# Up-projection of a ConvFFN in seven block products, with weight sums made by accumulating transfers

## The chip, the core and the metric

One core of a Trainium2 chip. The metric is the device time in microseconds of one execution. TensorE (PE) multiplies, VectorE (DVE), ScalarE (ACT) and GpSimd (POOL) work on tiles of 128 partitions, and SyncE (SP) issues most transfers. Each engine works through its own list of instructions in order; semaphores tie the lists together. A transfer that POOL issues goes through POOL's queue of descriptors, one that SP issues through SP's.

## What is computed

One layer of a hybrid decoder, for 512 prompt tokens and 8 single-token samples, 520 columns in all; the model width is 2048, the feed-forward width 5632. Cut to what matters here:

```python
h = rmsnorm(x, ln_mix_pre)
proj = h @ w_in                          # 2048 x 6160
...                                      # windowed attention and gated delta rule
mix = concatenate([att, dn_out]) @ w_out # 2048 x 2048
x = x + rmsnorm(mix, ln_mix_post)
h = rmsnorm(x, ln_ffn_pre)
up, ffn_new = causal_dwconv(h @ w_ffn_in, ffn_buf, ffn_conv_w)   # 2048 x 11264, width 3
gate, val = split(up + ffn_conv_b, 2)
f = (gelu(gate) * val) @ w_ffn_out                               # 5632 x 2048
x = x + rmsnorm(f, ln_ffn_post)
```

The sample caches, shifted by one row, are outputs too (128 copies of up to 1 MB from HBM to HBM).

## The kernel before

Features lie on partitions and tokens on columns. Every product of float32 values is made of three matmuls on a rounded high part and a low part: high × high, high × low and low × high. A weight tile `raw` (128 x 1024, 512 KB) is loaded by SP (line 111) and split in two steps of 128 x 512: a cast on ScalarE (line 127, `hi`) and a subtraction on VectorE (line 128, `lo`). The operand tiles `xa` and `xb` hold the high and low parts for 256 and 264 of the 520 columns (halves A and B). `gemm` (lines 152 to 162) issues the matmuls (line 160): for a tile of 128 output features 16 k-blocks × 3 × 2 halves = 96.

Stage 3, the FFN, begins when the output projection's last matmuls end, near 978 us. The loop takes 11 parts of four pairs. Pair f is gate tile f and value tile 44 + f: two `u_tile` calls (192 matmuls), whose results are scaled by R2, the row of inverse norms (line 1114), into tiles U. Then the depthwise convolution (first tap on ScalarE, line 1122; two taps each on VectorE, line 1124), the gelu (line 1133), gate times value on VectorE (line 1134), and the split of the product into the down-projection's operand. After each part the down-projection of the part before it runs (`ffn_out`, 384 matmuls) and adds into `yacc` (line 1188). The last part's down-projection goes by halves of the tokens, with the output's norm behind it. In the first part half A of the tokens goes first, so that the norm of half B (`mid2`) is made meanwhile. `shift` issues the cache copies on SP, three per pair.

What sets the order: a scheduler lays out each engine's list at build time, `HI()` marks work that is to go early, and weight units are prefetched two ahead (`LOOK`), through 3 raw, 5 high and 5 low buffers. Within an engine nothing overtakes.

Of the kernel before, what the change touches and what calls it, by code (L numbers as in the profile page):

```python
# [18 lines left out]
T = 520  # L19
NB4 = 11  # L20
TAGS = ("bankS", "bankT", "bankP", "bankX")
NCV = 5
NA, NB = 256, 264
# [16 lines left out]
def trunk(ctx, tc, I, O):  # L40
# [13 lines left out]
    wraw = enter(pool("wraw", 3))  # L54
    whi = enter(pool("whi", 5))
    wlo = enter(pool("wlo", 5))
    xsA = enter(pool("xsA", 16))
    xsB = enter(pool("xsB", 16))
    rrow = enter(pool("rrow", 1))
    dram = enter(tc.tile_pool(name="dram", bufs=1, space=bass.MemoryType.DRAM))  # L60
    gps = enter(tc.tile_pool(name="gps", bufs=2, space=bass.MemoryType.PSUM))
    sps = enter(tc.tile_pool(name="sps", bufs=4, space=bass.MemoryType.PSUM))
    turn = [0]

    def bank(tag=None):
# [26 lines left out]
    def ffn_units(p):  # L92
        u = []
        for f in range(4 * p, 4 * p + 4):
            u += [I["w_ffn_in"][f], I["w_ffn_in"][44 + f]]
        return u
    units += ffn_units(0) + ffn_units(0)
    for p in range(1, NP):
        units += ffn_units(p)
        units += [I["w_ffn_out"][p - 1, g].rearrange("p a b c -> p (a b) c") for g in range(4)]  # L100
    for _ in range(1):
        units += [I["w_ffn_out"][NP - 1, g].rearrange("p a b c -> p (a b) c") for g in range(4)]
# [5 lines left out]
    def emit_half(u, hf):  # L108
        with HI():
            raw = wraw.tile([128, 8, 128], F32, name="raw")  # L110
            lastw[0] = Q.dma_start(raw, units[u][:, hf * 8:hf * 8 + 8, :])
            if u >= len(units) - 4:
                # the last part is used twice: kept whole where the FFN's operand lay
                for q in range(4):
                    b = hf * 8 + q * 2
                    t = xsA.tile([128, 2, NA], F32R, name="xa") if q % 2 else xsB.tile([128, 2, NB], F32R, name="xb")
                    r = raw[:, q * 2:q * 2 + 2, :].rearrange("p a b -> p (a b)")
                    S.copy(t[:, 0, 0:256], r)  # L118
# [27 lines left out]
    def wblk(u, b):  # L146
        if u >= len(units) - 4:
            return wt[u, "b", b]
        hi, lo = wt[u, b // 4]
        return hi[:, b % 4, :], lo[:, b % 4, :]  # L150

    def gemm(blks, X, ks, parts="AB"):
        ps = gps.tile([128, 1024], F32, name="ps")
        n = len(ks)
        for i, k in enumerate(ks):
            wh, wl = wblk(*blks[i])
            for j, (w, b) in enumerate(((wh, 0), (wh, 1), (wl, 0))):
                for part in parts:
                    o, w_ = SEG[part]
                    PE.matmul(ps[:, 256 + o:256 + o + w_], w, X[k][part][:, b, :],  # L160
                              start=(i == 0 and j == 0), stop=(i == n - 1 and j == 2))
# [12 lines left out]
    def norm_row(dst, acc, n, wp):  # L174
        """dst = (mean over features + eps)^-1/2 replicated on all partitions, from squares added over k-tiles."""
        cn, k = (128, 2) if n == 256 else (88, 3)
# [70 lines left out]
    def bias_tables():  # L247
        rb = Pd.tile([32, H], F32, name="rb")
        B.dma_start(rb, I["rel_bias"])
        for dst, o, n in ((FD, 0, 640), (FS, 640, 400)):  # L250
# [4 lines left out]
            for a in range(0, n, 512):  # L255
# [3 lines left out]
                if n == 640:  # L259
                    # the scores of the prompt are kept with the opposite sign  # L260
# [25 lines left out]
    def b_tile(ct, ps, early):  # L286
        U = Pd.tile([128, 3 + T], F32, name="cv", bufs=NCV)
        V.memset(U[:, 0:3], 0.0)
        with HI():
            if early:  # L290
                S.copy(U[:, 3:], ps[:, 256:776])
                V.tensor_mul(U[:, 3:], U[:, 3:], R1)
            else:
                V.tensor_mul(U[:, 3:], ps[:, 256:776], R1)
# [31 lines left out]
    # gates: rows 0..7 beta, rows 32..39 the decay  # L326
# [5 lines left out]
    def gates(ps):  # L332
# [5 lines left out]
        with HI():  # L338
            S.copy(ga, ps[0:40, 256:776])
# [22 lines left out]
    def gate_cols():  # L362
# [4 lines left out]
        # the samples' decay and beta on all partitions  # L367
# [30 lines left out]
    def col_sums(c, o, keep):  # L398
        """squared norms of q (o = 0) or k (o = 4), tokens of a chunk on partitions."""
# [147 lines left out]
    def scan(c):  # L547
# [48 lines left out]
        # state  # L596
# [12 lines left out]
        # outputs  # L609
# [32 lines left out]
    def over_partitions(rows):  # L642
        """sums over the partitions, on all of them."""
# [4 lines left out]
    def sample_dn():  # L648
# [16 lines left out]
        # partitions (sample, value head, half of dk)  # L665
# [80 lines left out]
    def rows_of(src, last):  # L746
        """[128 d, (h, b)] -> DRAM [b][h][d]: the queries, or the last row of a shifted cache."""
# [636 lines left out]
```

## Time and profile before

| | |
|---|---|
| median of three runs | 2528.92 us (2526.8 to 2529.82) |
| profiled execution, span | 2524.7 us |
| TensorE busy | 2445.2 us (97%), 20080 matmuls |
| VectorE, ScalarE, POOL busy | 1478.5 (59%), 983.2 (39%), 206.7 us (8%) |
| moved by transfers | 469.46 MB, mean 186 GB/s |

The page gives the span of one execution and no other time of it; the runs lie 2 to 5 us above. In a row of the groups, the first number after the bar is the busy time of all, the second the mean of one in ns, and behind the next bar stands the engine's idle time just before them with what ended it. In a row of transfers the last number is the median time from issue to landing.

### The profile page before, as it was taken

The numbers are of one execution on the slowest core, as the hardware profiler recorded it, in microseconds if no ns is written. First come the engines' busy times: TensorE is split into PE (matmuls) and PEld (weight loads), VectorE is DVE, ScalarE is ACT, GpSimd is POOL, SyncE is SP. The second block draws the span as 40 slices with busy tenths as digits, with TensorE's granted clock in tenths as the row PEclk, the third lists the DMA queues.
The fourth block names the chain that finished last, engine by engine and source line by source line (L and its number), as shares of the span: only waits on it lengthen the run. The fifth ranks groups of instructions, "written<-read, shape, count | busy, mean of one in ns | idle before, by whom it ended". The sixth has DMA issues, their size and how long they took to land.

```text
span 2524.7 us, 49670 instructions
## 1 busy us (share of the span) xinstructions
PE 2445.2 (97%) x20080; PEld 2424.1 (96%) x20080; DVE 1478.5 (59%) x3246; ACT 983.2 (39%) x2096; POOL 206.7 (8%) x470
## 2 busy tenths in 40 slices
PE   8499999998999999999999999999999999999996
PEld 7499999997999999999999999999999999999996
DVE  7379755676896567855454544445454545444467
ACT  6153244683335556632232323232323323232344
POOL 1120211212110000100000000000000000000000
PEclk9799999999999999999999999999999999999998
DMA  5663532559984567965564736364555546463753
GB/s 184 148 226 126 186 114 87 164 187 242 247 218 132 187 197 228 328 228 194 184 203 143 244 134 217 128 242 145 208 179 190 197 155 231 138 226 115 264 170 103
DMA packets 119061, 469.46 MB, mean 186 GB/s; under 512 B 20032, under 2 KB 39408, under 8 KB 116784
## 3 DMA queue, kind: packets, MB, share of 16 engines
q1 hardware_dynamic: 93648, 393.60, 46.1%
q0 software_dynamic: 25184, 72.69, 10.5%
q8 instruction: 158, 2.59, 0.4%
q14 instruction: 71, 0.58, 0.1%
HBM read 432.40 MB, written 167.97 MB: 238 GB/s over the span
## 4 chain that ended last, share of the span: by engine, by line
PE 85%; DMA 5%; DVE 4%; ACT 3%; issue 2%; another core or an unknown queue 2%; POOL 0%; SPq 0%; DVEq 0%; POOLq 0%; ACTq 0%
PE ps L160 80%; DMA pc<-in_cache_k_dram 2%; ACT prod L697 1%; DVE dtmp L706 1%; DMA raw<-in_w_out_dram 1%; DMA X1D<-x 1%; DMA raw<-in_w_ffn_out_dram 1%; PE bankX L513 1%; PE bankP L513 1%; DVE lo L128 0%; DVE sjk L783 0%; PE bankT L513 0%; PE bankS L513 0%; DMA out_s_rec_dram<-pc 0%
## 5 line engine op out<-in xcount | busy, mean ns | idle before, releaser
L160 PE MATMUL ps<-xb,hi 128*128 128x264 f32 x4640 | 1191.2, 287 | 0.0
L160 PE MATMUL ps<-xa,hi 128*128 128x256 f32 x4640 | 1181.2, 283 | 9.1 <-ACT xa L170 8.6
L127 ACT CAST hi<-raw 128x512 fp32r<-128x512 f32 x868 | 533.5, 619 | 1194.0 <-PE ps L160 1120.3
L160 PEld LDWEIGHTS ps<-xa,hi 128*128 128x128 f32 x4640 | 861.4, 190 | 14.3 <-ACT xa L170 8.6
L160 PEld LDWEIGHTS ps<-xb,hi 128*128 128x128 f32 x4640 | 861.4, 189 | 5.0 <-issue 2.7
L128 DVE TENSOR_TENSOR lo<-raw,hi 128x512 fp32r<-128x512 f32 x868 | 594.3, 689 | 462.5 <-ACT hi L127 460.7
L160 PE MATMUL ps<-xb,lo 128*128 128x264 f32 x2320 | 666.3, 287 | 3.1 <-DVE lo L128 1.5
L160 PE MATMUL ps<-xa,lo 128*128 128x256 f32 x2320 | 656.8, 283 | 0.0
L160 PEld LDWEIGHTS ps<-xb,lo 128*128 128x128 f32 x2320 | 438.2, 189 | 6.2 <-DVE lo L128 3.6
L160 PEld LDWEIGHTS ps<-xa,lo 128*128 128x128 f32 x2320 | 439.1, 189 | 0.8 <-issue 0.5
L160 PE MATMUL ps<-actB,hi 128*128 128x264 f32 x1280 | 337.1, 284 | 0.0
L160 PE MATMUL ps<-actA,hi 128*128 128x256 f32 x1280 | 333.3, 281 | 0.6 <-DVE yacc L1188 0.6
L160 PEld LDWEIGHTS ps<-actA,hi 128*128 128x128 f32 x1280 | 241.1, 188 | 0.8 <-ACT xb L118 0.8
L160 PEld LDWEIGHTS ps<-actB,hi 128*128 128x128 f32 x1280 | 240.5, 188 | 0.0
L1188 DVE TENSOR_TENSOR yacc<-yacc,ps 128x520 f32<-128x520 f32 (+2 forms) x176 | 113.8, 646 | 182.0 <-PE ps L160 180.5
L160 PE MATMUL ps<-actB,lo 128*128 128x264 f32 x640 | 181.7, 284 | 0.0
L160 PE MATMUL ps<-actA,lo 128*128 128x256 f32 x640 | 180.2, 282 | 0.0
L1124 DVE SCALAR_TENSOR_TENSOR gt<-U,cols,gt 128x512 f32<-128x512 f32 x176 | 131.9, 750 | 23.0 <-ACT gt L1122 20.9
L1140 POOL COPY pu<-U 128x2 f32<-128x2 f32 x88 | 49.7, 565 | 1136.6 <-DVE U L1114 1136.4
L1114 DVE TENSOR_TENSOR U<-ps,R 128x520 f32<-128x520 f32 (+2 forms) x92 | 61.1, 664 | 137.8 <-PE ps L160 137.7
L160 PEld LDWEIGHTS ps<-actA,lo 128*128 128x128 f32 x640 | 121.4, 190 | 0.0
L160 PEld LDWEIGHTS ps<-actB,lo 128*128 128x128 f32 x640 | 120.4, 188 | 0.0
(517 smaller groups left out, 2156.9 us busy)
## 6 DMA issues: line engine op xcount, KB each, us to landing
raw<-in_w_ffn_in_dram SPq DMA_DIRECT2D x192, 512.0 KB, 4.0
raw<-in_w_in_dram SPq DMA_DIRECT2D x98, 512.0 KB, 4.8
raw<-in_w_ffn_out_dram SPq DMA_DIRECT2D x88, 512.0 KB, 4.2
raw<-in_w_out_dram SPq DMA_DIRECT2D x64, 512.0 KB, 4.0
pc<-in_cache_k_dram POOLq DMA_DIRECT2D x24, 512.0 KB, 8.7
pc<-in_cache_v_dram POOLq DMA_DIRECT2D x24, 512.0 KB, 8.5
pc<-in_state_rec_dram POOLq DMA_DIRECT2D x16, 512.0 KB, 4.9
out_s_win_k_dram<-in_cache_k_dram SPq DMA_DIRECT2D x8, 1020.0 KB, 9.9
```

The source lines that it names most:

```text
L127: S.copy(hi, r)
L128: V.tensor_sub(lo, r, hi.bitcast(F32))
L160: PE.matmul(ps[:, 256 + o:256 + o + w_], w, X[k][part][:, b, :], start=(i == 0 and j == 0), stop=(i == n - 1 and j == 2))
L513: PE.matmul(p[:, j * 128:j * 128 + 128], lhs(4 * g + j), rhs(4 * g + j), start=True, stop=True)
L697: S.activation(dst[:, k], src(k), AF.Identity, scale=kqd[:, j, pc * 8 + k:pc * 8 + k + 1])
L706: V.tensor_reduce(dst, pr.rearrange("p k v -> p v k"), axis=AX.X, op=OP.add)
L1114: return V.tensor_mul(u, p, R2[:, o:o + w])
L1124: V.scalar_tensor_tensor(dst, U[:, j:j + 512], fwc(j, f), dst, op0=OP.mult, op1=OP.add)
L1140: G.tensor_copy(pu[:, s, i, :], U[:, 512:514])
L1188: ev = V.tensor_add(yacc[:, m, o:o + w], yacc[:, m, o:o + w], ps[:, 256 + o:256 + o + w])
```

## The change

The weights of pair f are seen as a 2 x 2 block matrix: rows are halves of the 2048 input features (8 k-blocks each), columns are gate and value: B11, B21 for the gate, B12, B22 for the value. The tokens' operand is a 2 x 2 block matrix too: rows are the halves of tokens (now 260 and 260), columns the feature halves. The four result blocks are made of seven products instead of eight. The operand sums A11, A12, A22, S1 to S4 are made once, in `mid2`, with R2 multiplied in; the weight sums are made for each pair. A product is 24 matmuls of 128 x 260 (line 1235).

The weight sums are transfers of POOL that add in flight (line 1153): the raw tile X holds a block, is cast and subtracted (`hl`, lines 1138 to 1142, now on 128 x 1024 at once), then the next block is added onto it from HBM, and so on: B11, + B12 (T1), + B22 (T2), + B21 (the last). Y holds B22, then B22 + B12. That is four adding transfers a pair.

Pairs below 16 have their two gate products (A11 with B11, A12 with B21) made ahead of the loop and kept in HBM (`PD`); they stand beside the making of half B's operands. Such a pair has five products in the loop, the others have seven.

The gated results go to HBM (`ACT`, line 1256) and the whole down-projection follows as sweeps of two parts, with PSUM adding over eight k-blocks (line 1413). The last part's weights are loaded twice. The gate times value multiply goes from VectorE to POOL (line 1255).

```diff
-NA, NB = 256, 264
+NA, NB = 260, 260
+EARLY = 16
...
-        norm_row(R2[:, o:o + w], acc3[:, :, :w], w, wk)
+        r2 = wk.tile([128, NB], F32, name="r2", bufs=1)
+        norm_row(r2, acc3, w, wk)
...
+        for i in range(4):
+            h1, h2 = scale(i), scale(4 + i)
+            put("A22", i, h2, xsB)
+            s = wk.tile([128, 2, w], F32, name="sd", bufs=2)
+            V.tensor_sub(s, h1, h2)
+            yield
+            a1, a2 = whole("A11", i), whole("A12", i)
+            V.tensor_sub(h1, a1, h1)
+            put("S3", i, h1, sxp)
+            put("S1", i, s, xsB)
...
+    wrx = enter(pool("wrx", 2))
+    whl = enter(pool("whl", 4))
...
+    def hl(raw):
+        t = whl.tile([128, 2, 8, 128], F32R, name="hl")
+        S.copy(t[:, 0], raw)
+        V.tensor_sub(t[:, 1], raw, t[:, 0].bitcast(F32))
+        return t
...
+    def wadd(t, src):
+        B.dma_start(t, src, accum_op=OP.add)
...
+    def pair_jobs(f):
+        def b11():
+            pre(f)
+            X = PRE[f][0]
+            t = hl(X)
+            wadd(X, wblock(f, 0, 1))
+            return t
...
+        def t1():
+            pre(f + 1)
+            X = PRE[f][0]
+            t = hl(X)
+            wadd(X, wblock(f, 1, 1))
+            return t
+
+        def t2():
+            X = PRE[f][0]
+            t = hl(X)
+            wadd(X, wblock(f, 1, 0))
+            return t
...
+        if f < EARLY:
+            jobs.extend([b22, t1, t2, last(1), last(0)])
+        else:
+            jobs.extend([b11, b22, t1, t2, last(1), last(2), last(0)])
...
+    JLOOK = 3
...
+    def product(p, X, first=True):
+        w = next_w()
+        n = 0
+        for a, b in ((0, (0, 1)), (1, (0,))):
+            for k in range(8):
+                for c in b:
+                    PE.matmul(p[:, 0:NA], w[:, a, k, :], X[k][:, c, :], start=first and n == 0, stop=n == 23,
...
-        V.tensor_mul(gt, gt, vt)
...
+        G.tensor_mul(gt, gt, vt)
+        Q.dma_start(ACT[f], gt)
...
+        pe = bank("bankX")
+        product(pe, XC["S4"])
+        v = small("v")
+        with HI():
+            S.copy(v, pe[:, :NA])
+        pd = fbank("bd")
+        product(pd, XC["S1"])
+        pb = fbank("bb")
+        product(pb, XC["S2"])
+        u2, u3 = small("u2", 1), small("u3", 1)
+        with HI():
+            V.tensor_add(u2, u, pb[:, :NA])
+            G.tensor_sub(v, v, u2)
+        pc = fbank("bc")
+        product(pc, XC["S3"])
...
+        product(pc, XC["A22"], first=False)
+        with HI():
+            V.tensor_add(gb_, u2, pc[:, :NA])
+        gated(f, Ug, Uv, pst)
+        shift(3)
...
+    sweeps = [(2 * i, 2 * i + 1) for i in range(5)] + [(10,)]
+    runs = [(s, "AB") for s in sweeps[:-1]] + [(sweeps[-1], "A"), (sweeps[-1], "B")]
```

How the instructions stand on the engines that the weights pass through. In the rows DMAHW is a wait for a transfer of SP, DMASW one for a transfer of POOL. First ScalarE's list in the middle of the FFN, before; `hi<-raw` is the weights' cast and `gt` the convolution and the gelu:

```order
L127 CAST hi<-raw 128x512 [waits DMAHW7_49,PE_49,Activation_49]
L127 CAST hi<-raw 128x512 [waits PE_49,Activation_49]
L127 CAST hi<-raw 128x512 [waits DMAHW3_49,PE_49,Activation_49]
L1122 ACTIVATE gt<-U,cols 128x512 [waits DVE_49,Pool_49]
L127 CAST hi<-raw 128x512 [waits PE_49,Activation_49]
L1133 ACTIVATE gt<-gt 128x512 [waits DVE_49]
L127 CAST hi<-raw 128x512 [waits DMAHW4_49,PE_49,Activation_49]
```

And the same list in the change, one of the pairs from 16 on; `rx` is X, `ry` is Y, `rz` is B21:

```order
L1341 COPY U<-ba 128x260 [waits PE_49]
L1243 ACTIVATE gt<-U,cols 128x512 [waits DMAHW3_49,DVE_49,Activation_49]
L1243 ACTIVATE gt<-U,cols 128x512 [waits Pool_49]
L1318 COPY u<-ba 128x260 [waits PE_49]
L1254 ACTIVATE gt<-gt 128x512 [waits DVE_49]
L1323 COPY v<-bankX 128x260 [waits PE_49]
L1140 CAST hl<-rx 128x1024 [waits DMASW3_49]
L1140 CAST hl<-rx 128x1024 [waits DMASW5_49]
L1140 CAST hl<-ry 128x1024 [waits DMASW4_49]
L1140 CAST hl<-rz 128x1024 [waits DMAHW5_49]
L1140 CAST hl<-rx 128x1024 [waits DMASW6_49,DVE_49,PE_49]
L1140 CAST hl<-rx 128x1024 [waits DMAHW3_49,DVE_49,PE_49]
```

Before, the casts wait for SP's loads and for free buffers and lie between the convolution's steps. Now the casts of T1 and T2 stand directly behind one another and behind the copy of S4's result, and three of the six wait for transfers of POOL.

ScalarE's list in the change for a pair below 16, from the gelu of the pair before it to the next pair's:

```order
L1254 ACTIVATE gt<-gt 128x512 [waits DVE_49]
L1140 CAST hl<-rx 128x1024 [waits DMASW1_49,Activation_49]
L1140 CAST hl<-ry 128x1024 [waits DMASW0_49,Activation_49]
L1140 CAST hl<-rx 128x1024 [waits DMASW3_49,PE_49]
L1140 CAST hl<-ry 128x1024 [waits DMAHW2_49,PE_49,Activation_49]
L1140 CAST hl<-rx 128x1024 [waits DMASW2_49,DVE_49,PE_49]
L1323 COPY v<-bankX 128x260 [waits PE_49,Pool_49]
L1243 ACTIVATE gt<-U,cols 128x512 [waits DMAHW1_49,DMAHW0_49,DVE_49]
```

Its casts are T2, Y's second, X's last, then B22 and T1 of the next pair; here T2 stands behind a gelu, and the next pair's B22, a plain load, behind X's last.

POOL's list before, from one pair to the next:

```order
L1118 MEMSET U 128x2 [waits DVE_49,Activation_49,Pool_49]
L1140 COPY pu<-U 128x2 [waits DVE_49]
L1141 COPY su<-U 128x8
```

And in the change, one of the pairs from 16 on:

```order
L1255 TENSOR_TENSOR gt<-gt 128x512 [waits DMAHW6_49,Activation_49]
L1153 DMA rx<-in_w_ffn_in_dram 128x1024 [waits DMASW7_49,DVE_49]
L1153 DMA rx<-in_w_ffn_in_dram 128x1024 [waits DMASW1_49,DVE_49]
L1331 TENSOR_TENSOR v<-v,u_19039 128x260 [waits DVE_49]
L1258 COPY pu<-U 128x2 [waits DVE_49]
L1259 COPY su<-U 128x8
L1153 DMA rx<-in_w_ffn_in_dram 128x1024 [waits DMAHW3_49,DMASW6_49,DVE_49]
L1153 DMA ry<-in_w_ffn_in_dram 128x1024 [waits DMAHW6_49,DMASW4_49,DVE_49]
```

POOL now multiplies gate by value, and behind that issues the adding transfers, each of which waits for VectorE's subtraction of the same tile and for the transfer before it.

More of the change, by code (lines that the diff above doesn't have):

```diff
@@ L1015, in trunk @@
     X1D = dram.tile([128, KT, T], F32, name="X1D")
-    R2 = rrow.tile([128, T], F32, name="R")
-    H2 = [{} for _ in range(KT)]
     def mid(part, also):
@@ new lines, in mid2, with put @@
+        if part == "A":
+            for g in range(8):
+                h = scale(g)
+                for j in range(2):
+                    t = xsA.tile([128, 2, w], F32R, name="xa")
+                    split(t, h[:, j], 0, w)
+                    XC["A11" if g < 4 else "A12"][2 * (g % 4) + j] = t
+                yield
+            return
+        def put(name, i, src, pl):
+            for j in range(2):
+                t = pl.tile([128, 2, w], F32R, name="xb" if pl is xsB else "xs")
+                split(t, src[:, j], 0, w)
+                XC[name][2 * i + j] = t
@@ L1080, in after @@
             step(g, n)
+    XC = {n: [None] * 8 for n in ("A11", "A12", "A22", "S1", "S2", "S3", "S4")}
     mix_split("A", mxA)
@@ L1089, in trunk @@
     next(ga)
-    b_ = mid("B", lambda m, ev: after(ev, ga, m % 2))
+    b_ = mid("B", lambda m, ev: after(ev, ga, 1))
     run_all(ga)
     Pmb.close()
-    Pw2 = ExitStack()
-    gb = mid2("B", *b_, enter(pool("wk2"), Pw2))
-    next(gb)
+    W1.close()
+    Gs.close()
     Pmx.close()
     P1s.close()
-    fu = enter(pool("fu", side="right"))
-    fwc = lambda j, f: col(C_FW + j * FT + f)
-    act = {}
-    def u_tile(f, parts, U, early=False):
-        u = next_unit()
-        ps = gemm([(u, k) for k in range(KT)], H2, range(KT), parts=parts)
-        o = SEG[parts[0]][0]
-        w = sum(SEG[p][1] for p in parts)
-        with HI():
-            u, p = U[:, 2 + o:2 + o + w], ps[:, 256 + o:256 + o + w]
-            if early:
-                S.copy(u, p)
-                p = u
-            return V.tensor_mul(u, p, R2[:, o:o + w])
@@ L1121, in conv_u, with fbank @@
+    def fbank(tag):
+        return fps.tile([128, 512], F32, name=tag)
     def conv_u(f, U, dst):
@@ L1165, in part_end @@
         S.activation(y[:, 0], y[:, 0], AF.Gelu_apprx_tanh)
[L1166 to L1170 removed]
+        V.tensor_mul(sact[:, 4 * p:4 * p + 4], y[:, 0], y[:, 1])
         Q.dma_start(O["p_ffn"][p], pu)
         Q.dma_start(O["s_ffn"][p], su)
[L1174 to L1176 removed]
+    for f in range(0, EARLY, 2):
+        pp = [fbank(("ba", "bb")[i]) for i in range(2)]
+        for k, n in enumerate(("A11", "A12")):
+            for i in range(2):
+                product(pp[i], XC[n], first=k == 0)
+                with HI():
+                    t = wk2.tile([128, NA], F32, name="sp", bufs=2)
+                    S.copy(t, pp[i][:, :NA])
+                    Q.dma_start(PD[f + i][:, k], t)
+                step(gb, 1)
@@ new lines, in trunk, with load_act @@
+    Fps.close()
+    Fs.close()
+    gp2 = enter(tc.tile_pool(name="gp2", bufs=2, space=bass.MemoryType.PSUM))
+    yac = enter(pool("yac", side="right"))
+    yacc = yac.tile([128, KT, T], F32, name="yacc")
+    fo = enter(pool("fo", side="right"))
+    act = {}
+    def load_act(f):
+        r = fo.tile([128, T], F32, name="ar", bufs=3)
+        Q.dma_start(r[:, 0:512], ACT[f])
+        G.tensor_copy(r[:, 512:520], sact[:, f])
+        act[f] = {}
+        for part, pl, n in (("A", xsA, "xa"), ("B", xsB, "xb")):
+            o, w = SEG[part]
+            act[f][part] = t = pl.tile([128, 2, w], F32R, name=n)
+            split(t, r[:, o:o + w], 0, w)
@@ L1193, in trunk @@
-    Us0 = [new_u() for _ in range(8)]
-    for i in range(8):
-        f = (i // 2) + 44 * (i % 2)
-        after((u_tile(f, "A", Us0[i], i < 2),), gb, 1)
-    run_all(gb)
-    Pw2.close()
-    fw = enter(pool("fw", side="right"))
-    yac = enter(pool("yac", side="right"))
-    yacc = yac.tile([128, KT, T], F32, name="yacc")
-    ps0 = part_begin(0)
-    for i in range(8):
-        f = (i // 2) + 44 * (i % 2)
-        u_tile(f, "B", Us0[i], i < 2)
-        if i % 2:
-            pair(i // 2, Us0[i - 1], Us0[i], ps0)
-        shift(1)
@@ L1220, in trunk @@
+    for f in range(8):
+        load_act(f)
+    for i, s in enumerate(sweeps[:-1]):
+        for q in sweeps[i + 1]:
+            for f in range(4 * q, 4 * q + 4):
+                load_act(f)
+        ffn_out(s, "AB")
+        shift(8)
     shift(len(copies))
@@ L1237, in f @@
             S.activation(y, y, AF.Identity, scale=col(C_LN4 + m))
-            if also and m in range(1,16,2):
+            if also and m in range(1, 16, 2):
                 with tc.issue_after(lastev[0]):
```

296 lines of the change are left out of this document (193 added, 103 removed).

## The prediction

> **What bounds the kernel now.** I read the page's first lines, then the chain of waits, then the stretches of time. The engines' busy time and the chain's shares by engine:
>
> ```profile
> span 2524.7 us, 49670 instructions
> PE 2445.2 (97%) x20080; PEld 2424.1 (96%) x20080; DVE 1478.5 (59%) x3246; ACT 983.2 (39%) x2096; POOL 206.7 (8%) x470
> PE 85%; DMA 5%; DVE 4%; ACT 3%; issue 2%; another core or an unknown queue 2%; POOL 0%; SPq 0%; DVEq 0%; POOLq 0%; ACTq 0%
> ```
>
> The chain from 1000 us on, in order of time (its longest pieces), and busy time by stretch (length, then PE, PEld, DVE, ACT, POOL with counts, granted clock, DMA share, GB/s):
>
> ```profile
> 1043.65 1385.58 PE ps L160 x11559
> ...
> 900.00:1050.00 150.00, 148.26 (x1209) 146.13 (x1208) 114.62 (x216) 90.87 (x180) 6.88 (x13) 1.00 0.75 245
> 1260.00:2400.00 1140.00, 1140.00 (x9517) 1140.00 (x9516) 552.07 (x967) 348.04 (x605) 55.08 (x204) 1.00 0.54 186
> ```
>
> From 1043.65 us TensorE runs 1386 us on end. Over 1260 to 2400 us it is busy in every microsecond at clock 1.00, with VectorE at 48% and ScalarE at 31%. So a matmul taken out there is worth its full time, and any wait put before one costs its full time. One matmul of about 260 columns is 1140.00 / 9517 = 119.8 ns; a product of 24 is 2.875 us.
>
> **Removed.** A pair of column tiles falls from 192 matmuls to 7 × 24 = 168. Over 44 pairs that is 1056 × 0.1198 = 126.5 us, from 44 × 192 × 0.1198 = 1012 us of up-projection. The columns per matmul and the down-projection's count stay. The 126.5 us is the whole gain to be had.
>
> **Added: a serial chain of weight sums.** Durations that it needs (columns: count, busy us and mean ns of one, idle before):
>
> ```profile
> L127 ACT CAST hi<-raw 128x512 fp32r<-128x512 f32 x868 | 533.5, 619 | 1194.0 <-PE ps L160 1120.3
> L118 ACT CAST xb<-raw 128x256 fp32r<-128x256 f32 x16 | 6.5, 405 | 8.9 <-DMA raw<-in_w_ffn_out_dram 8.9
> L473 DVE TENSOR_TENSOR b<-b,b 128x1024 f32<-128x1024 f32 x4 | 4.9, 1220 | 2.6 <-DMA b<-BRD 2.6
> L1122 ACT ACTIVATE gt<-U,cols 128x512 f32<-128x512 f32 x88 | 71.7, 816 | 30.2 <-DVE U L1114 30.1
> L1133 ACT ACTIVATE gt<-gt 128x512 f32<-128x512 f32 x44 | 27.9, 633 | 2.7 <-DVE gt L1124 2.7
> L1124 DVE SCALAR_TENSOR_TENSOR gt<-U,cols,gt 128x512 f32<-128x512 f32 x176 | 131.9, 750 | 23.0 <-ACT gt L1122 20.9
> L1188 DVE TENSOR_TENSOR yacc<-yacc,ps 128x264 f32<-128x264 f32 x16 | 6.8, 427 | 1.7 <-PE ps L160 1.3
> L1112 ACT COPY U<-ps x4: 367/371/383, 986.6 to 1038.5; 128x256 f32<-128x256 f32 x2, 128x264 f32<-128x264 f32 x2
> ```
>
> A cast grows 619 − 405 = 214 ns per 256 columns, so the new 128x1024 cast (line 1140) is about 619 + 428 = 1.05 us. Its subtraction (line 1141) is 1.22 us by the row of that shape. The gate's tile is split, summed by a transfer, split again, three times over: no sum may be issued before the subtraction has read the tile, and the next cast needs the sum landed. Call L the time from such a transfer's issue to its landing. ScalarE takes its work in order, so whatever stands behind a late cast is late too.
>
> *A late pair (f ≥ 16), from the start of its A11 product.* A11 and S4 end at 5.75. ScalarE copies S4's result (0.37) and only then casts T1, ready at 6.12 + 1.05 = 7.17, where S1 can start (it would be due at 5.75). T1's subtraction ends at 8.39, the sum lands at 8.39 + L, T2 is cast at 9.44 + L. S2 waits for that; S2, S3, A12 and A22 follow, 11.5 us. Period 20.94 + L, against 20.1 us of matmuls and 23.0 before. POOL's gate multiply stands in front of this sum on its queue: the gelu before it ends near 5.2 (first tap 0.82, three taps 2.25, gelu 0.63, behind gb's add 0.43), so it is hidden up to 3.2 us, beyond which it adds. On SP the store of the gated tile (line 1256) waits for that multiply, with the next pair's loads behind it; their first cast stands behind X's last one, some 10 us on, more than a load takes.
>
> *An early pair (f < 16), from the start of S4.* PE runs S4 of the next pair and A22 of this one, 5.75. Then gb's add 0.43, first tap 0.82, three taps 2.25 and the gelu 0.63 pass before the cast of T2 (1.05), which stands behind that gelu on ScalarE: about 11.0. Subtraction to 12.2; the sum lands at 12.2 + L. Then X's last cast and, behind it, B22 of the next pair: 2.1 us. Period 14.3 + L with 14.4 us of matmuls in it, so nothing of L is hidden.
>
> The up-projection is thus 32 × 2.875 = 92 (products made beforehand) + 16 × (14.3 + L) + 28 × (20.94 + L) = 907 + 44 L.
>
> **What L is.** No accumulating transfer is in the trace of before. The nearest rows are plain 512 KB transfers (KB, median us to landing):
>
> ```profile
> raw<-in_w_ffn_in_dram SPq DMA_DIRECT2D x192, 512.0 KB, 4.0
> pc<-in_cache_k_dram POOLq DMA_DIRECT2D x24, 512.0 KB, 8.7
> pc<-in_state_rec_dram POOLq DMA_DIRECT2D x16, 512.0 KB, 4.9
> ATD<-b POOLq DMA_DIRECT2D x4, 512.0 KB, 3.4
> out_s_win_k_dram<-in_cache_k_dram SPq DMA_DIRECT2D x8, 1020.0 KB, 9.9
> BRD<-jk POOLq DMA_DIRECT2D x1, 16.0 KB, 1.7
> ...
> q1 hardware_dynamic: 93648, 393.60, 46.1%
> ```
>
> POOL's queue, from which the sums go, landed 512 KB in 3.4 us at best and 8.7 us under load. A gain (an L below a plain transfer's) is excluded by the sum reading as much from HBM as the copy does and then writing. I start from the state's 4.9 us (HBM to SBUF, as here, beside other traffic) and add one more pass of the tile, since the old value has to be fetched: q1 moved 393.60 MB in 46.1% of 2524.7 us, 338 GB/s, so 512 KB is 1.55 us. L = 6.4, bounds 3.4 and 8.7. With 6.4 the up-projection is 907 + 282 = 1189, or +177 on 1012.
>
> The Trainium skill, "Collectives: The Full Stack", Part 3, "Why ReduceScatter is half of AllGather", says that the add itself is free there and that the second source read halves the rate; by it, as an estimate, the rate part of a plain transfer doubles, which is the 1.55 us taken above. No run here shows it yet.
>
> The third sum must also land in time: after S2's start the queue owes another subtraction and L before the last cast. The X chain alone is 4 casts + 3 subtractions + 3 L = 7.9 + 3 L a late pair, less than 20.94 + L up to L = 6.5. So 6.4 is just under the point where all three sums count and not one.
>
> **The clock.** TensorE will stand still 28 times for about L − 0.6 = 5.8 us in the late pairs, and 16 times for about L in two pieces. Such a gap in the trace of before, early in the span:
>
> ```profile
> 78.00:84.00 6.00, 1.76 (x15) 1.52 (x14) 0.00 (x0) 0.00 (x0) 0.00 (x0) 0.91 0.51 88
> 84.00:90.00 6.00, 3.21 (x16) 3.21 (x17) 2.51 (x4) 1.66 (x3) 0.00 (x0) 0.52 0.63 125
> 90.00:96.00 6.00, 6.00 (x52) 6.00 (x51) 0.00 (x0) 0.62 (x1) 0.00 (x0) 1.00 0.51 87
> ```
>
> After some 7 us with hardly a matmul the granted clock is 0.52 and 16 matmuls take 3.21 / 16 = 200 ns, 16 × 80 ns = 1.3 us lost. The lower end is 0 (shorter gaps than this one may leave the clock alone), the upper 28 × 1.3 = 36; I take 20, since the late gaps of 5.8 are near the 7 us, but not that long.
>
> The Trainium skill, "TensorE: Matmul & The Clock Gate", Part 1, gives about 3.4 us of idleness for half clock and as long to recover, which speaks against this change: by it every late gap halves the clock and the term is the upper one. The 84 to 90 row agrees in kind (0.52).
>
> **The other edges.**
>
> ```profile
> L1060 DVE TENSOR_TENSOR x<-x,xb 128x528 f32<-128x528 f32 x8 | 5.6, 704 | 0.1
> raw<-in_w_ffn_out_dram SPq DMA_DIRECT2D x88, 512.0 KB, 4.2
> ```
>
> - Start: the new weight tiles lie over old ones, so the first split waits for the last output-projection matmul: a cast and a subtraction, +3 (0 if the weights' pool were free, 6 if the load of 4.0 comes behind it too).
> - Products made beforehand: VectorE owes 32 splits × 1.22 = 39, half B's residual and square sums 8 × 3 × 0.70 = 17, and 4 × (18 × 0.43 + 4 × 0.70) = 42 of operand sums, 98 us, plus the norms' waits, against 92 of matmuls: +10 (6 to 20).
> - Between the projections TensorE has nothing: the last pair's add, taps and gelu (4.1), POOL's multiply (1 to 3), its store (3 to 4), reload (4) and split (1): +13.
> - The first sweep wants three loads at once (4.2 each, partly side by side) and the last part's weights come twice: +7. Fewer yacc adds lie beside a busy TensorE and count nothing, as do the operands' R2 scaling and POOL's copies.
>
> Together +33. **Sum:** −1012 + 1189 + 20 + 33 = +230, on 2524.7 gives 2755. The runs lie 2 to 5 us above the profile's span (median 2528.92), so **2759 us**. Without L the sum is −1012 + 907 + 33 + 44 L = −72 + 44 L: the change pays below L = 1.6 us.
>
> **Rivals.**
> - *All three sums decide.* Above L = 6.5 a late pair takes 7.9 + 3 L. For: an early pair moves six 512 KB tiles, two small ones and three cache copies of 1020 KB, 6.8 MB in some 21 us, 320 GB/s against the 338 above, and the cache rows' 8.7 us came under load. Against: 4.0 us for the weights' loads beside the same cache copies. L = 8: 92 + 16 × 22.3 + 28 × 31.9 = 1342, +330, with 36 and 33: 2928. L = 8.7: 2998.
> - *Sums as quick as plain transfers.* L = 3.4 to 4.5, for which the 3.4 and 4.0 rows speak: 907 + 44 × 3.9 = 1079, +67, with 33 and 10 for the clock: 2639. At 3.4 and no clock loss 2607.
> - *The sums are never waited for (not slower).* If T1's and X's sums land within 1.6 us of issue, or the casts run further ahead than ScalarE's written order lets them, TensorE keeps its 20.1 and 14.4 us: 92 + 16 × 14.4 + 28 × 20.9 = 907, with 33: 2457; it decides from L = 1.6 down. Against it: 16 KB took 1.7 us on this queue, 512 KB never under 3.4.
>
> **Numbers.** Forecast (L 4.5 to 7.2) 0.61; three sums 0.20; plain transfers 0.13; not waited for 0.06. The range goes from the plain transfers' lower end, 2607, to L near 8.7, 2985: 2607 to 2985 leaves out the third rival and the tail above. A measurement of this kernel cannot tell less than about 0.2% from no change. Faster 0.05, same 0.02, slower 0.93.
>
> **What would show it.** Right: the landing of rx and ry transfers from POOL near 6.4 us; TensorE's idle time ahead of line 1235 ended by ScalarE's cast (line 1140), 28 times 5 to 6 us before S2 and once more before S4 or A22 in early pairs; a period of 27.4 us in late pairs and 20.7 in early ones, read off the gelu's starts; granted clock below 1.00 in the late stretch; some 13 us of empty TensorE between lines 1235 and 1413. Wrong: idle time ended by VectorE or POOL there (the multiply, then, or the splits bind), PE busy above 95% of the up-projection (third rival), or a gap before the third sum as long as before the second (first rival).

## The result, and the profile after

The changed kernel takes 2982.52 us (median; 2979.94 to 2992.44) against 2529.37 us beside it: a ratio of 1.1797, 95% interval 1.1774 to 1.182. The forecast was slower, 2759 us, with 2607 to 2985 as its range. The direction is right and the range holds the median at its upper end (one of the four executions lies above it); the most likely case was 224 us too low.

The first lines of the page, the chain's shares and the stretches of the FFN (length, then PE, PEld, DVE, ACT and POOL busy with counts, granted clock, DMA share, GB/s):

```profile
span 2980.9 us, 47943 instructions
PE 2507.7 (84%) x19078; PEld 2465.1 (83%) x19078; DVE 1572.4 (53%) x3130; ACT 1083.7 (36%) x2032; POOL 436.2 (15%) x778
DMA 26%; PE 23%; issue 6%; DVE 5%; ACT 3%; POOL 1%; POOLq 0%; DVEq 0%; SPq 0%; ACTq 0%
...
984.60:1088.70 104.10, 97.05 (x776) 95.83 (x777) 87.90 (x151) 59.58 (x111) 4.00 (x3) 0.96 0.84 286
1136.00:1534.00 398.00, 275.97 (x1832) 269.32 (x1833) 173.97 (x262) 116.67 (x143) 97.92 (x185) 0.83 0.90 243
1582.00:2401.00 819.00, 612.51 (x4220) 600.89 (x4218) 339.49 (x480) 254.86 (x331) 162.32 (x305) 0.84 0.78 218
2500.00:2700.00 200.00, 200.00 (x1667) 200.00 (x1666) 78.73 (x103) 46.89 (x67) 3.89 (x16) 1.00 0.36 114
```

The chain was 85% TensorE and is now led by transfers, 26%. TensorE is still full in the sweeps of the down-projection (2500 to 2700), but in the pairs (the second and third stretch) it is busy 69% and 75% of the time, at a granted clock of 0.83 and 0.84. No other compute engine is near full there; the transfer engines are busy 0.90 of the early pairs and 0.78 of the late ones.

The transfers behind it, by queue (packets, MB, share of 16 engines) and by issue (KB, median us to landing); the rows of POOLq are the sums:

```profile
q1 hardware_dynamic: 110352, 406.32, 39.6%
q0 software_dynamic: 50528, 164.98, 26.7%
...
rx<-in_w_ffn_in_dram POOLq DMA_DIRECT2D x132, 512.0 KB, 6.4
rx<-in_w_ffn_in_dram SPq DMA_DIRECT2D x55, 512.0 KB, 12.7
ry<-in_w_ffn_in_dram POOLq DMA_DIRECT2D x44, 512.0 KB, 12.0
```

One late pair in order of time (start, us, engine, line, count, and in brackets the idle time before it with what ended it):

```profile
2001.05 0.89 POOL L1153 DMA_DIRECT2D rx<-in_w_ffn_in_dram  x1 [1.39 <-DVE hl L1141]
...
2010.92 1.04 ACT L1140 CAST hl<-rx 128x1024 fp32r<-128x1024 f32 x1 [3.19 <-DMA rx<-in_w_ffn_in_dram]
...
2012.02 5.38 PE L1235 MATMUL bd<-xb,hl 128*128 128x260 f32 x24 [4.70 <-ACT hl L1140]
2013.52 0.88 POOL L1153 DMA_DIRECT2D rx<-in_w_ffn_in_dram  x1 [6.06 <-DVE hl L1141]
2019.09 1.04 ACT L1140 CAST hl<-rx 128x1024 fp32r<-128x1024 f32 x1 [7.13 <-DMA rx<-in_w_ffn_in_dram]
...
2020.19 3.65 PE L1235 MATMUL bb<-xs,hl 128*128 128x260 f32 x16 [2.79 <-ACT hl L1140]
...
2021.70 0.88 POOL L1153 DMA_DIRECT2D rx<-in_w_ffn_in_dram  x1 [7.29 <-DVE hl L1141]
...
2024.07 0.60 SPq L884 DMA_DIRECT2D out_s_win_v_dram<-in_cache_v_dram  x1
2025.01 0.51 SPq L884 DMA_DIRECT2D out_s_win_k_dram<-in_cache_k_dram  x1
2025.58 0.57 SPq L884 DMA_DIRECT2D out_s_win_v_dram<-in_cache_v_dram  x1
...
2028.31 2.00 ACT L1140 CAST hl<-rx 128x1024 fp32r<-128x1024 f32 x2 [6.26 <-DVE u L1335]
...
2031.20 1.22 DVE L1141 TENSOR_TENSOR hl<-rx,hl 128x1024 fp32r<-128x1024 f32 x1
...
2032.72 0.89 POOL L1153 DMA_DIRECT2D rx<-in_w_ffn_in_dram  x1 [1.39 <-DVE hl L1141]
```

From one first sum to the next (2001.05 to 2032.72) there is nothing but X's chain: sum, cast, subtraction, sum, cast, subtraction, sum, the two casts at 2028.31 (X's last and B11 of the next pair), and B11's subtraction. TensorE waits twice in it, 4.70 us for T1 and 2.79 us for T2. The forecast had 1.4 and 5.8 us there and one landing in the period. Over 25 late pairs TensorE waited 123.4 us before S1 and 80.4 us before S2, which is 4.9 and 3.2 us a pair: the larger wait is the one that the forecast had as the smaller. Taken issue by issue over the late pairs, X's three sums land after 10.6, 5.6 and 6.4 us (medians). The first is the slow one: three cache copies (line 884) are issued 7 to 9 us ahead of it.

The period of the pairs is read from the gelu's first and last start: 16 early pairs, then 26 late ones.

```profile
L1254 ACT ACTIVATE gt<-gt x16: 627/630/635, 1136.0 to 1534.0; 128x512 f32<-128x512 f32 x16
...
L1254 ACT ACTIVATE gt<-gt x26: 630/634/636, 1582.1 to 2401.5; 128x512 f32<-128x512 f32 x26
```

(1534.0 − 1136.0) / 15 = 26.5 us and (2401.5 − 1582.1) / 25 = 32.8 us, against 20.7 and 27.3 in the forecast: 16 × 5.8 + 28 × 5.5 = 247 us. With the 20 us for the clock, which lie inside these periods, taken off, that is 227, the difference of 224 to within a few us. In total the rest of the sum needs no repair. Between the projections TensorE waited 10.94 and 2.50 us, where 13 were forecast:

```profile
2422.95 3.11 PE L1235 MATMUL bc<-xb,hl 128*128 128x260 f32 x24 [0.91 <-DVE u L1335]
2437.01 0.80 PE L1413 MATMUL ps<-xa,hl 128*128 128x260 f32 x2 [10.94 <-ACT xa L147]
...
2442.48 0.51 PE L1413 MATMUL ps<-xa,hl 128*128 128x260 f32 x2 [2.50 <-ACT xa L147]
```

### The profile page after: what moved, and what is told of

It reads as the page before. It is cut to its first block, busy times and chain, and to the rows that moved or that the text cites. A ratio compares the mean times of both kernels' runs of the same rounds, so it can differ in the third digit from the quotient of the medians.

```text
span 2980.9 us, 47943 instructions
## 1 busy us (share of the span) xinstructions
PE 2507.7 (84%) x19078; PEld 2465.1 (83%) x19078; DVE 1572.4 (53%) x3130; ACT 1083.7 (36%) x2032; POOL 436.2 (15%) x778
## 3 DMA queue, kind: packets, MB, share of 16 engines
q0 software_dynamic: 50528, 164.98, 26.7%
## 4 chain that ended last, share of the span: by engine, by line
DMA 26%; PE 23%; issue 6%; DVE 5%; ACT 3%; POOL 1%; POOLq 0%; DVEq 0%; SPq 0%; ACTq 0%
DMA rx<-in_w_ffn_in_dram 24%; PE ps L1413 16%; PE bb L1235 4%; DVE hl L1141 3%; ACT hl L1140 3%; PE bc L1235 2%; DMA PD<-sp 1%; PE ba L1235 1%; POOL v L1331 1%; DMA ar<-ACT 0%; DMA ry<-in_w_ffn_in_dram 0%; DVE u L1330 0%; DVE gt L1245 0%; DMA out_yT_dram<-U 0%; DVE yacc L1468 0%
## 5 line engine op out<-in xcount | busy, mean ns | idle before, releaser
L1413 PE MATMUL ps<-xa,hl 128*128 128x260 f32 x2112 | 487.5, 284 | 14.1 <-ACT xa L147 13.4
L1413 PE MATMUL ps<-xb,hl 128*128 128x260 f32 x2112 | 489.2, 285 | 2.7 <-DVE yacc L1420 2.7
L140 PE MATMUL ps<-xa,hi 128*128 128x260 f32 x1824 | 470.6, 289 | 9.4 <-ACT xa L150 8.6
L140 PE MATMUL ps<-xb,hi 128*128 128x260 f32 x1824 | 470.9, 290 | 0.0
L1413 PEld LDWEIGHTS ps<-xa,hl 128*128 128x128 f32 x2112 | 387.1, 190 | 15.5 <-ACT xa L147 13.9
L1413 PEld LDWEIGHTS ps<-xb,hl 128*128 128x128 f32 x2112 | 387.2, 190 | 3.7 <-ACT hl L1140 2.0
L140 PEld LDWEIGHTS ps<-xa,hi 128*128 128x128 f32 x1824 | 338.7, 191 | 13.6 <-ACT xa L150 8.6
L140 PEld LDWEIGHTS ps<-xb,hi 128*128 128x128 f32 x1824 | 338.2, 190 | 4.8 <-issue 2.4
L109 ACT CAST hi<-raw 128x512 fp32r<-128x512 f32 x324 | 197.6, 618 | 271.5 <-PE ps L140 233.6
L110 DVE TENSOR_TENSOR lo<-raw,hi 128x512 fp32r<-128x512 f32 x324 | 220.9, 689 | 122.2 <-ACT hi L109 120.2
```

The lines of the kernel that those rows point to most:

```text
L109: S.copy(hi, r)
L110: V.tensor_sub(lo, r, hi.bitcast(F32))
L140: PE.matmul(ps[:, PO + o:PO + o + w_], w, X[k][part][:, b, :], start=(i == 0 and j == 0), stop=(i == n - 1 and j == 2))
L1413: PE.matmul(ps[:, PO + o_:PO + o_ + w_], t[:, a, i * 4 + k, :], act[4 * p + k][part][:, b, :], start=n == 0, stop=n == last)
```

## Experiments

The theory after the result: in each pair TensorE waits for a chain of landings, and the cache copies lengthen one of them. The rivals: the addition itself is dear, the queue shared with Y's sum is, the slowed clock is, or the transfer engines are simply full.

### Without the sums

```diff
     def wadd(t, src):
-        B.dma_start(t, src, accum_op=OP.add)
+        pass
```

> Leaves the 176 adding transfers out: T1, T2, the last X and the second Y are then plain blocks, so the up-projection's values are not the reference's; every cast, subtraction, product and store stays. Theory (the sums' landing sets the pair, and the clock falls in the gaps they make): a late pair drops from 32.4 us to 20 to 22, an early one from 26.5 to 14.5 to 17, so the time falls to 2500 to 2580 us and the granted clock in the pairs is near 1.00. Rival (ScalarE's order, POOL's multiply or the splits set the pair, the sums only lie beside them): late pairs stay above 26 us and the time above 2750.

Measured: 2453.13 us, ratio 0.9698 (0.9683 to 0.9713). The gelu's rows:

```profile
L1254 ACT ACTIVATE gt<-gt x16: 632/633/635, 1125.2 to 1339.8; 128x512 f32<-128x512 f32 x16
...
L1254 ACT ACTIVATE gt<-gt x26: 632/634/637, 1376.8 to 1880.4; 128x512 f32<-128x512 f32 x26
```

14.3 us an early pair and 20.1 a late one, the time of their matmuls. So the sums cost 2982 − 2453 = 529 us, and all the rest of the change (ScalarE's order, POOL's multiply, the splits, the stores, the sweeps) takes 76 us off. The forecast's sum without L was −72. The scheduler lays the engines' lists anew when the program changes: only the next run has those of the change, and what the new order is worth by itself in this run and the later ones was not measured apart.

### Copies in the sums' place

```diff
     def wadd(t, src):
-        B.dma_start(t, src, accum_op=OP.add)
+        B.dma_start(t, src)
```

> The same 176 transfers from the same queue at the same places and of the same size, but as plain copies over the tile instead of additions (values are not the reference's). Theory A (the addition itself is dear: it takes the transfer engines about 3.0 us a tile against 1.5 for a copy, worked out from the queues' shares, and two sums stand on the queue at once): landing falls from 6.4 and 12.0 to about 4 and 6, a late pair to 25 to 28 us, the time to 2700 to 2800. Theory B (any transfer in that place costs as much, the fixed part of the landing decides): time 2900 to 2980.

Measured: 2840.27 us, ratio 1.1234 (1.1211 to 1.1258), between the two theories. In the FFN the order of every engine's instructions is that of the change. The queue's row here, and in the run without sums:

```profile
q0 software_dynamic: 50528, 164.98, 19.9%
```

```profile
q0 software_dynamic: 25184, 72.69, 10.8%
```

An addition takes (26.7% × 2980.9 − 10.8% × 2449.5) / 176 = 3.0 us of all the transfer engines, a copy (19.9% × 2839.2 − 264.5) / 176 = 1.7 us. X's second and third transfers land after 3.9 and 4.1 us instead of 5.6 and 6.4, the first after 10.9 as before. So adding costs 142 us, but with mere copies in the same places 387 us of the 529 remain: that is what a transfer in these places costs, its traffic included, whether it adds or not.

### The cache copies out of the pairs

```diff
         gated(f, Ug, Uv, pst)
-        shift(3)
...
-        shift(8)
+        shift(24)
```

> The cache copies that the pairs issue (three a pair) go into the down-projection instead (24 a sweep for 8). Theory (they lengthen the sums): landing falls from 6.4 and 12.0 towards 5.4 and 10, 1 to 2 us off each pair, the time to 2880 to 2940, nothing given back, since the transfer engines are busy 36% in the down-projection. Rival (the sums' own rate on their queue decides): 2965 to 2990.

Measured: 2979.59 us, ratio 1.179 (1.1758 to 1.1822), no change, but not for the rival's reason:

```profile
L1254 ACT ACTIVATE gt<-gt x26: 621/626/632, 1567.1 to 2260.5; 128x512 f32<-128x512 f32 x26
...
ry<-in_w_ffn_in_dram POOLq DMA_DIRECT2D x44, 512.0 KB, 6.3
...
2304.46 34.92 PE ps L1412 x288
...
2344.53 11.45 DMA out_s_win_k_dram<-in_cache_k_dram
2356.00 25.47 DMA out_s_win_k_dram<-in_cache_k_dram
2381.49 22.47 DMA out_s_win_k_dram<-in_cache_k_dram
```

A late pair falls to (2260.5 − 1567.1) / 25 = 27.7 us; X's first sum lands after 5.7 us in the median instead of 10.6, the other two after 5.6 and 6.5 as before, and the sum of Y after 6.3 us instead of 12.0. That 27.7 is near the 27.3 of the forecast is chance. In the pair that begins with the first sum at 1911.92 and ends with the next at 1939.50, three landings, four casts and three subtractions of X's chain still follow one another, where the forecast had one landing. The early pairs hardly gain, 25.1 us against 26.5; with one copy a pair left in (the next run) they take 22.8, and why is open. The gain is then lost in the down-projection: the last three rows, from the chain of waits, are part of 24 copies in one block on SP, ahead of the next weights, for some 60 us after each sweep.

### The copies spread out

```diff
         gated(f, Ug, Uv, pst)
-        shift(3)
+        shift(1)
...
+                if len(parts) == 2:
+                    shift(2)
...
-        shift(8)
```

> One cache copy a pair instead of three, and two after each half group of the down-projection (80 in all) instead of eight after each sweep. With the copies out of the pairs a late pair took 27.5 us instead of 32.7, but the time did not fall, since 24 copies in one block stood ahead of the down-projection's weights on SP. Theory (the copies' traffic costs the pairs about 5 us each, and spread out it costs the down-projection little): late pairs 28 to 30 us, early ones 25 to 26, no gap over 5 us in the down-projection, 2860 to 2920 us. Rival (the copies cost the same wherever they lie, some 3 us of all the transfer engines each): 2950 to 2990.

Measured: 2853.98 us, ratio 1.1273 (1.1251 to 1.1296), a little under the theory's range. Late pairs 29.3 us, early ones 22.8, lower than the 25 to 26 expected. Two thirds of the copies moved, 129 us gained: where the copies stand is worth about that much, with what they cost in the down-projection taken off.

### The clock

Extra matmuls on ready operands ahead of the products that TensorE waits for:

```diff
+    def warm():
+        p = bank("bankS")
+        for i in range(24):
+            PE.matmul(p[:, 0:NA], XC["A11"][0][:, 0, 0:128], XC["A11"][1][:, 0, :], start=i == 0, stop=i == 23)
...
+        if f >= EARLY:
+            warm()
         pd = fbank("bd")
         product(pd, XC["S1"])
+        warm()
         pb = fbank("bb")
```

> 24 extra matmuls on ready operands, into a PSUM bank that nothing reads, ahead of the products before which TensorE waits (S1 and S2 in late pairs, S4 and S2 in early ones); the result is unchanged. Some 2100 matmuls more, all meant to lie in idle time. Theory (the gaps lower the granted clock and the slow matmuls behind them cost about 140 us over the pairs): most of that comes back, the time falls to 2860 to 2930 with the clock near 1.00. Rival (slow matmuls lie beside the next sum's landing anyway, so they cost nothing): the clock rises and the time stays within 2960 to 3010.

Measured: 2988.08 us, ratio 1.1807 (1.1785 to 1.183); the rival's outcome. The same stretch of the late pairs in the change and in this run:

```profile
1550.00:2400.00 850.00, 635.15 (x4372) 623.18 (x4371) 351.56 (x494) 263.76 (x342) 168.96 (x315) 0.84 0.78 218
```

```profile
1550.00:2400.00 850.00, 720.36 (x5437) 704.58 (x5436) 354.65 (x500) 266.00 (x346) 174.43 (x321) 0.92 0.79 221
```

The clock rises from 0.84 to 0.92 and nothing is gained. The slow matmuls of S1 (5.38 us for 24, above) lie beside the next sum's landing: while X's chain sets the pair, TensorE's speed has no price.

### Without Y's sums

```diff
             t = hl(Y)
-            wadd(Y, wblock(f, 0, 1))
             return t
```

> Leaves out the 44 sums of Y alone (B22 + B12 is then plain B22, values are not the reference's); X's three sums and all copies stay. Theory (Y's sum is issued right behind X's first and third ones and shares the queue with them, so X's first sum lands after 9 us rather than 6): late pairs fall by 2 to 4 us, early ones by 2 to 4, the time to 2840 to 2920. Rival (X's own three sums and the copies set it, Y's lies beside them): within 20 us of 2982.

Measured: 2958.17 us, ratio 1.169 (1.1666 to 1.1714); the theory fell. Late pairs stay at 32.8 us, and X's first sum still lands after 10.6 us there; only the early pairs fall, from 26.5 to 24.8, which is the 24 us gained. What delays it is the copies ahead of it (5.7 us with none in the pairs), not Y's sum beside it.

### X's next chain begun earlier

A11 of the next pair is multiplied ahead of A22 of this one (its loop change, with A11's own result tile, is left out here):

```diff
-            jobs.extend([b11, b22, t1, t2, last(1), last(2), last(0)])
+            if f == EARLY:
+                jobs.append(b11)
+            NB11[f] = b11
+            jobs.extend([b22, t1, t2, last(1), last(2)])
+            if f + 1 < NFP:
+                jobs.append(lambda: NB11[f + 1]())
+            jobs.append(last(0))
```

> The adding transfers as in the change, but from pair 16 on the product A11 with B11 of the next pair stands ahead of A22 of this one (its result in a bank that is free), so B11's cast and the first sum behind it no longer wait for the last sum of the pair before. The result is unchanged. Theory (from pair to pair the sums of X form one chain, three landings in a row with splits between them, and that chain is the period of a late pair): two of the three landings then lie side by side, late pairs fall from 32.7 to 24 to 28 us, the time to 2760 to 2860; early pairs stay. Rival (the queue and the transfer engines are what is full, about 12 us of sums, 9 us of copies and 5 us of loads a pair): late pairs stay above 31 us and the time above 2940.

Measured: 2953.05 us, ratio 1.1667 (1.1647 to 1.1687). Late pairs 31.6 us: the rival's outcome.

```profile
2014.47 0.75 SPq L884 DMA_DIRECT2D out_s_win_v_dram<-in_cache_v_dram  x1
2015.51 0.88 POOL L1153 DMA_DIRECT2D rx<-in_w_ffn_in_dram  x1 [2.52 <-DVE hl L1141]
2015.57 0.51 SPq L884 DMA_DIRECT2D out_s_win_k_dram<-in_cache_k_dram  x1
...
2016.13 0.59 SPq L884 DMA_DIRECT2D out_s_win_v_dram<-in_cache_v_dram  x1
...
2032.51 1.04 ACT L1140 CAST hl<-rx 128x1024 fp32r<-128x1024 f32 x1 [8.43 <-DMA rx<-in_w_ffn_in_dram]
```

The first sum leaves sooner, at 2015.51, and flies 17 us (16.6 in the median), beside the third sum and in the midst of the same three copies, of which one is issued 1 us before it and two within 0.7 us behind it. With both edits at once:

> The two single edits together: B11's cast of the next pair ahead (its first sum went out 10 us sooner, but landed after 16.5 us behind the three cache copies, so late pairs only fell to 31.0 us), and one cache copy a pair with two per half group of the down-projection (late pairs 29.2 us, 2854 us by itself). Theory (the copies fill the transfer engines for some 9 us a pair at the very place where the early sum would fly; without them the chain is two landings long): late pairs 23 to 26 us, early ones about 23, the time 2680 to 2780. Rival (four sums of about 3 us of all the transfer engines and the loads are themselves what is full, or another wait follows): late pairs 27.5 to 29.5, the time 2800 to 2860.

Measured: 2769.59 us, ratio 1.093 (1.0912 to 1.0948), in the theory's range; late pairs 26.4 us, just above it, early ones 22.8. Each edit alone gained 129 and 29 us, together 213. Chain and copies hide one another: a shorter chain is worth little while the copies hold its transfer back. What is left, 26.4 against 20.1 us, is two landings with some 9 us of casts and subtractions: X's second sum with 5.7 us and its first with 11.3 (medians), which now flies beside the third and one copy.

### The sums on VectorE

```diff
-    def wadd(t, src):
-        B.dma_start(t, src, accum_op=OP.add)
+    def wadd(e, t, src):
+        e.tensor_add(t, t, src)
...
+        X, W, Y, Z = (wload(n, wblock(f, *b)) for n, b in (("rx", (0, 0)), ("ro", (0, 1)), ("ro", (1, 1)), ("ro", (1, 0))))
...
+            wadd(V, X, Y)
+            wadd(V, Y, W)
...
+            wadd(V, X, Z)
```

> The same sums made by VectorE: all four blocks of a pair are loaded plainly by SP, and four 128x1024 additions of about 1.22 us each take the place of the four adding transfers; the raw tiles share the same space in another way. The result is the reference's but for rounding. Theory (only the transfers' landing was dear): late pairs 20 to 21.5 us with VectorE some 90% busy, early ones 16 to 18, VectorE-bound; the time 2480 to 2545 us. Rival (a serial chain of split, sum, split costs as much on an engine, behind ScalarE's order): over 2600.

Measured: 2474.67 us, ratio 0.9786 (0.9765 to 0.9807), below both kernels. Late pairs 20.1 us, TensorE without a gap; early ones 16.1, where VectorE is the bound. Its stretch of early pairs, and of late ones:

```profile
1120.00:1340.00 220.00, 197.48 (x1584) 192.63 (x1584) 205.60 (x277) 100.31 (x123) 88.48 (x110) 0.99 0.97 345
1360.00:1900.00 540.00, 540.00 (x4500) 539.80 (x4500) 510.28 (x620) 275.47 (x356) 175.72 (x219) 1.00 0.83 281
```

The chain of splits and sums has the same links; only the link of some 6 us has become one of 1.22 us, and the blocks to be added are loaded beforehand. The transfer engines are busy 0.97 and 0.83 of these stretches, more than in the change (0.90 and 0.78), so it was not their being full that set the pairs there. With two of the four sums on POOL (`wadd(G, X, W)` and `wadd(G, Y, W)`):

> As the one before, but X's first sum and Y's sum are made on POOL (some 2.5 us each), the two others on VectorE. Theory: VectorE falls to some 80% in late and 95% in early pairs, late pairs 20 to 21, early ones 14.5 to 16; the time 2455 to 2510 us, below the kernel before. Rival (POOL's additions are slower beside VectorE, or stand ahead of its multiply and delay X): 2530 to 2620.

Measured: 2547.79 us, ratio 1.0067 (1.0052 to 1.0082); the rival.

```profile
L1249 ACT ACTIVATE gt<-gt x16: 624/627/637, 1119.5 to 1426.1; 128x512 f32<-128x512 f32 x16
```

An early pair takes (1426.1 − 1119.5) / 15 = 20.4 us instead of 16.1, a late one 20.4 instead of 20.1: nearly all of the 73 us is lost in the early pairs. VectorE has two additions less a pair and yet is busier in the late pairs, 552.62 of 560 us against 510.28 of 540. The groups of VectorE in the late pairs with all sums on VectorE, and then with two on POOL (busy us, mean ns):

```profile
L1141 DVE TENSOR_TENSOR hl<-rx,hl 128x1024 fp32r<-128x1024 f32 x98 | 143.8, 1467 | 21.3 <-ACT hl L1140 19.9
L1141 DVE TENSOR_TENSOR hl<-ro,hl 128x1024 fp32r<-128x1024 f32 x74 | 90.2, 1219 | 0.0
...
L1240 DVE SCALAR_TENSOR_TENSOR gt<-U,cols,gt 128x512 f32<-128x512 f32 x97 | 70.4, 747 | 0.0
```

```profile
L1141 DVE TENSOR_TENSOR hl<-ro,hl 128x1024 fp32r<-128x1024 f32 x81 | 166.8, 2060 | 0.0
L1240 DVE SCALAR_TENSOR_TENSOR gt<-U,cols,gt 128x512 f32<-128x512 f32 x108 | 132.9, 1280 | 0.0
L1141 DVE TENSOR_TENSOR hl<-rx,hl 128x1024 fp32r<-128x1024 f32 x107 | 130.4, 1219 | 1.9
```

The subtraction of the `ro` tiles takes 2060 instead of 1219 ns, the convolution tap 1280 instead of 747, while the subtraction of X is back at 1219 from 1467. What is slow is whatever lies beside POOL's tiles: counted one by one, the 75 taps of this run that overlap a two-operand operation of POOL take 1916 ns in the mean, the 101 others 743. In the early pairs the tap's mean is 1239 ns, and VectorE's subtractions, taps and additions are 45% of the chain of waits, against 22% with all sums on VectorE; POOL's additions are 1% of it. With nothing of two tiles left on POOL (`V.tensor_mul(gt, gt, vt)`, `V.tensor_sub(v, v, u2)`):

> As the version with the sums on VectorE, but gate times value (128x512) and the difference v - u2 (128x260) go from POOL to VectorE as well. Theory (VectorE's subtraction took 1467 instead of 1220 ns in one place, and 2060 where POOL added tiles: two-operand work on POOL and on VectorE hold each other up): VectorE takes 0.7 + 0.4 us more a pair but loses the slow subtractions, so early pairs fall below 16.1 us and the time to 2455 to 2472. Rival (VectorE is full, every operation put on it costs its own time): early pairs 17 to 17.5 us, the time 2490 to 2510.

Measured: 2472.53 us, ratio 0.9775 (0.9755 to 0.9795), not to be told from 2474.67.

```profile
L1141 DVE TENSOR_TENSOR hl<-rx,hl 128x1024 fp32r<-128x1024 f32 x98 | 119.3, 1217 | 2.5 <-ACT hl L1140 2.5
```

The mean of this subtraction falls from 1467 to 1217 ns, as the theory has it, but the early pairs do not get shorter (16.4 us), so the theory fell there, and the rival's 17 us and more did not come either: what VectorE gains it spends on the two operations it took over. Last, the copies taken out of the early pairs of the version with the sums on VectorE (`shift(3 if f >= EARLY else 0)`, one per half group later):

> The version with the sums on VectorE (2474.67 us), with no cache copies in the pairs below 16 and one per half group of the down-projection in their place. Theory (in those pairs the transfer engines are 97% busy beside a VectorE that is 93% busy, and the loads of a pair come late): early pairs fall from 16.1 to about 15, the time to 2450 to 2466. Rival (VectorE alone is the bound there): early pairs stay at 16 us and the time within 6 us of 2475.

Measured: 2482.52 us, ratio 0.9805 (0.9791 to 0.982). The early pairs, with VectorE and the transfer engines in the fourth and the eighth figure:

```profile
1105.00:1360.00 255.00, 235.85 (x1887) 229.17 (x1886) 246.67 (x326) 118.70 (x149) 111.89 (x126) 0.99 0.51 158
```

They take 16.4 us, not fewer than before, though the transfer engines' share falls from 0.97 to 0.51; VectorE, busy 246.67 of 255 us, is the bound. The time is 8 us higher, but the intervals of the two ratios overlap, so it can't be told whether the copies cost anything where they were put.

## Why the prediction was right or wrong

- **The gain and the edges: right.** −1012 + 907 + 33 gave −72 without the sums' landing; the run without sums has −76. The price of the rival in which the sums are not waited for, 2457 us, is what that run measures (2453.13). The wait between the projections came as forecast too, 10.94 + 2.50 against 13.
- **L: right in size.** 6.4 us was taken for a landing, and sums without copies ahead of them land after 5.6 to 6.5 us (medians). Of the two parts, the plain landing was taken as 4.9 us, where X's copies landed after 3.9 and 4.1; the extra pass was put at 1.55 us and measures 3.0 − 1.7 = 1.3 of engine time. By the rule cited from the Trainium skill's "Collectives: The Full Stack", Part 3, the second read halves the rate; the trace agrees roughly, 3.0 against 1.7 us is 1.8 times.
- **The step that failed: "Period 20.94 + L" and "14.3 + L", one landing to a pair.** A late pair pays for all three landings of X, as B11 of the next pair is cast behind X's last, and its first sum is behind that; the last two rows of ScalarE's list for a late pair had that order. This is the rival that had 0.20. Its formula, with the landings measured, gives 7.9 + 10.6 + 5.6 + 6.4 = 30.5 us, 2.3 short of the 32.8. In the pair shown, 0.9 us of it is B11's subtraction, which stands behind X's last one and two additions (its cast is done at 2030.31, it starts at 2031.20), and 0.3 us passes three times between the end of a subtraction and the issue of its sum (2032.42 to 2032.72). In early pairs the sum that makes T2 out of T1 was taken as hidden under the convolution; it lands after 10.6 us in the median and ScalarE waits for it, so two landings count there as well.
- **Why the condition was missed.** The rival was tied to L above 6.5. The run without copies in the pairs shows that this limit was too high: its landings are 5.7, 5.6 and 6.5 us and its late pair 27.7, which leaves 9.9 us beside the three landings where 7.9 was summed. With 9.9 the rival begins at L = 5.5, below the 6.4 that was taken. The copies then made it dear: counted in the forecast as load on the engines over the whole pair, they are issued in a block of three directly ahead of X's first sum and add 4.9 us to it. With fewer copies beside the sums the time falls by 129 us. A term was averaged over a pair where its place in the pair decided.
- **The range: held in part by luck.** The forecast's own formula reaches only −72 + 20 + 44 × 8.7 = +331, or 2860 us, at L = 8.7. The end at 2985 is about what the rival's formula gives for three landings of 8.6 us each (its sum for 8.7 is 2998). The three measured have a mean of 7.5; late pairs take 32.8 us where that end has 33.7, early ones 26.5 where it has 22.9.
- **The clock: agreed in kind, priced wrongly.** The granted clock fell to 0.84 in the late pairs, and raising it to 0.92 did not change the time. The rule cited from the Trainium skill's "TensorE: Matmul & The Clock Gate", Part 1, that gaps of this length bring half clock, agrees with S1's 24 matmuls in 5.38 us behind a wait of 4.70 (224 ns each, where 120 is the full rate). The forecast added a slow matmul's extra time to the sum; beside a landing that ends later it costs nothing.

## What to carry to other kernels

When a chain of steps crosses a transfer several times, write down the whole loop from one turn to the next, across the boundary of the iteration, before calling a link hidden; an engine that is busy 97% before the change tells nothing of it. A transfer of some 6 us in a chain is worth replacing by an engine operation of 1.2 us wherever an engine has room: that turned +18% into −2%. Bulk copies that are free beside a full TensorE are not free directly ahead of a transfer that someone waits for; look at where in the loop they are issued.

## What the runs showed that was not expected

- Two-operand work on POOL slows VectorE: with POOL adding 128x1024 tiles, VectorE's convolution tap went from 747 to 1280 ns in the mean of the late pairs (1916 where it overlaps POOL's operation, 743 where it does not) and one of its subtractions from 1219 to 2060, and moving two of four additions off VectorE made the kernel 73 us slower.
- An adding transfer of 512 KB holds the transfer engines 3.0 us, a copy from the same queue 1.7 us, and X's second, which has no copies of the caches ahead of it, lands after 5.6 and 3.9 us.
- A small store can fly 19 us behind copies. In the changed kernel the results of the products made beforehand (130 KB) are stored by SP in 32 pieces that land after 3.7 us in the median; the slowest is issued at 1087.07, behind cache copies issued at 1081.84 and 1085.07, and ScalarE, which has two buffers for them, waits for the landing; this piece of the chain of waits stands at the start of the pairs:

```profile
1087.07 18.99 DMA PD<-sp
```

It remains open how far the version with two landings (26.4 us a late pair) would fall with no copies in the pairs at all, and whether VectorE's early pairs could be relieved by fewer products made beforehand; neither was tried.
